# Splits of the local attention's results moved to other steps of the latent attention

## The chip, the cores and the metric

The kernel runs on one core of a Trainium2 chip. A core has five engines that work side by side, each through its own list of instructions in order: TensorE (PE in the profile, with PEld for its weight loads), VectorE (DVE), ScalarE (ACT), GpSimd (POOL) and SyncE (SP), which here issues nearly all transfers between HBM and the on-chip memory SBUF. Matmul results go to PSUM banks, which DVE and ACT read. Engines wait for each other through semaphores. The metric is the device time of one execution in microseconds (us); the time before is 1336.53 us, the median of three runs.

## The reference

One decoder block on a sequence of 1024 positions with a model width of 1024, all in float32. Two attentions run side by side and are mixed:

```
h = RMSNorm(x); p = h @ w_in          # queries, keys, values, latents, gates
A = sliding-window attention (window 128, 8 heads, 2 key/value heads, sinks, rotary)
B = multi-head latent attention (8 heads, low-rank q and kv, causal, blocks of 128 queries)
y = sigmoid(gate_a) * (A @ w_o_swa) + sigmoid(gate_b) * (B @ w_o_mla)
x = x + y @ w_out
x = x + SwiGLU(RMSNorm(x)); final RMSNorm
```

The change concerns `A @ w_o_swa`, the output product of the local (sliding-window) attention. The kernel computes it during the latent attention.

## The kernel before, in words

Every large matrix product is made of three matmuls on float32r operands (`mm3`, L168 to L174): each operand is split into a high part, the value rounded by a cast, and a low part, the rest. `split` (L160 to L166) is one cast on ACT (L163) and one subtraction on DVE (L166). So each matmul operand that does not come out split costs ACT and DVE one instruction each per 128x512 piece.

The local attention leaves its result in HBM as `oa_d`, four pieces of 128x1024 (a group `g` of channels and a half `sh` of the sequence each). `load_oa(g, sh)` (L1261) takes buffers and issues the load of one piece into `oar`; `split_oa(g, sh, c)` (L1265) splits one half of the piece, 128x512, into `wv`, where the output product (`mix_a`, `oA` in the profile) reads it. There are four loads and eight splits in all. The weights of that product come through `wr` and are split into another `wv` of 128x1024.

Latent attention first makes its operands: key products (`prod_k`, `k`), query products (`prod_q`, `q`) and value blocks (`prod_v`, `v`). Then it runs 64 steps, eight heads by eight blocks of 128 queries in the order 2, 3, 6, 7, 0, 1, 4, 5. Step t is written like this:

1. `scores(t + 2)` (L1180 to L1208): the matmuls of two steps ahead into `scb` (two PSUM slots), the masked row maximum `nmb` on DVE (L1204), the exponential `p` on ACT (L1205), and on POOL the reciprocal `denb` (L1206) and the scaling of `p` (L1207).
2. The products of probabilities and values (`pv`, `ob`) that have become due.
3. In steps 0 to 3 one of the four last key products, (2, 0) to (3, 1), whose split result `kns` is stored to `kn_d` and loaded again for later heads. In steps 5 and 6, and in some of each later head's, half an output product `mix_a`.
4. `transposes(t)`: PE transposes `p` into `pTb`, which is split into `pth` and `ptl`.
5. Loads and splits for the output products: the part that the change touches.

Steps 0 and 1 have their scores before the loop. The whole order of PE, ACT, DVE and SP in this stage is not the written one: outside of the stretches that are marked as written by hand, a scheduler sets each engine's order when the program is built, from the written order and estimated times, with casts inside the loop's last part held in their written order among each other (`held`). The order then stands fixed in each engine's list, and each engine waits at the head of its list.

Before the loop, `load_oa(0, 0)` and `load_oa(1, 0)` stand ahead of the last query product `prod_q(3, ...)`. `ps1` has four PSUM banks that `q`, `k`, `v`, `pTb`, `ob` and `oA` share.

Of the kernel before, what the change touches and what calls it, by code (L numbers as in the profile page):

```python
# [89 lines left out]
def hybrid_block_kernel(  # L90
# [39 lines left out]
    def psum_phase(name, bufs):  # L130
        if psum:
            psum.pop("cm").close()
        psum["cm"] = ExitStack()
        psum["x"] = psum["cm"].enter_context(tc.tile_pool(name=name, bufs=bufs, space=PSUM))
# [9 lines left out]
    def U(name, dt=F32, shape=(P, 1024)):  # L144
        return pool.tile(list(shape), dt, tag="u", name=uid(name))

    def V(name, dt=F32, shape=(P, 4, 512)):
        return vpool.tile(list(shape), dt, tag="v", name=uid(name))
# [12 lines left out]
    def split(hi, lo, src, eng=None):  # L161

        i = nc.scalar.copy(hi, src)  # L163
        if held[0]:
            tc.keep_in_program_order(i)
        (eng or nc.vector).tensor_tensor(lo, src, hi.bitcast(F32), op=ALU.subtract)  # L166

    def mm3(ps, pairs, first=True, last=True, go_on=False):  # L168

        n = len(pairs)  # L170
        for i, ((ah, al), (bh, bl)) in enumerate(pairs):
            nc.tensor.matmul(ps, ah, bh, start=first and i == 0, stop=False, skip_group_check=go_on)  # L172
            nc.tensor.matmul(ps, ah, bl, start=False, stop=False, skip_group_check=go_on)  # L173
            nc.tensor.matmul(ps, al, bh, start=False, stop=last and i == n - 1, skip_group_check=go_on)  # L174
# [10 lines left out]
    def half(s):  # L185
        return slice(512 * s, 512 * s + 512)
# [189 lines left out]
    for g in range(NG):  # L376
        t = V("khd", F32R, (P, 2, S))
# [486 lines left out]
    for b in range(NB):  # L864
# [17 lines left out]
        t = U("lat", F32, (P, C_CKV))  # L882
# [100 lines left out]
    for i, b in enumerate((4, 5, 6, 7, 0, 1, 2, 3)):  # L983
        ps = P1("kl", (P, KVL))
        mm3(ps, [(hT(k, blk(b)), (wkl[k // 4][0][:, k % 4], wkl[k // 4][1][:, k % 4])) for k in range(NK)])
        t = U("lat", F32, (P, 2, KVL))
# [137 lines left out]
    def prod_q(j, s, k0=0, n=3):  # L1124
        w = wuq[j]
        if k0 == 0:
            q_ps[0] = (P1 if j > 1 else PX)("q")
        ps = q_ps[0]
        mm3(ps, [((w[:, 0, k], w[:, 1, k]), (cq[k][0][:, half(s)], cq[k][1][:, half(s)])) for k in range(k0, k0 + n)],
            k0 == 0, k0 + n == 3)  # L1130
        if k0 + n < 3:
            return
        t = U("qns", F32R, (P, 2, 512)) if j else None
        outs = [(t[:, 0], t[:, 1], ps)] if j else [
            (qT[u][0:64, 0, half(s)], qT[u][0:64, 1, half(s)], ps[64 * u:64 * u + 64]) for u in range(2)]
        for hi, lo, src in outs:
            nc.scalar.activation(hi, src, AF.Copy, scale=-SC_B)
            nc.vector.scalar_tensor_tensor(lo, src, -SC_B, hi.bitcast(F32), op0=ALU.mult, op1=ALU.subtract)
        if j:
            nc.sync.dma_start(qn_d[j][:, :, half(s)], t.bitcast(F32))  # L1140
# [13 lines left out]
    def prod_v(b):  # L1154
        ps = P1("v")
        mm3(ps, [((ckv[k][0][:, blk(b)], ckv[k][1][:, blk(b)]), (wv[0][:, k], wv[1][:, k])) for k in range(2)])
        if b % 2 == 0:
            t = V("vM", F32R, (P, 2, NH, P))
            vM.extend([t[:, 0], t[:, 1]])
        split(vM[b][:, :, 0:HD], vM[b][:, :, HD:P], ps.rearrange("p (h d) -> p h d", d=HD))  # L1160

    def load_k(h):
        nc.sync.dma_start(kT[h % 3][0:64].bitcast(F32), kn_d[h // 2, 64 * (h % 2):64 * (h % 2) + 64])
# [16 lines left out]
    def step(t):  # L1180
        return t // NB, order[t % NB]

    def scores(t):
        h, n = step(t)
        w = (n + 1) * P
        sc = PX("scb", (P, 1024))
        qh, ql = (qT[h][0:QK, i] for i in range(2))
        kh, kl = (kT[h % 3][0:QK, i] for i in range(2))
        cw = 320 if w == 640 else 512
        for c0 in range(0, w, cw):  # L1190
            c1 = min(c0 + cw, w)
            kc = slice(c0, c1)
            o = slice(c0 // cw * 512, c0 // cw * 512 + c1 - c0)
            nc.tensor.matmul(sc[:, o], qh[:, blk(n)], kh[:, kc], start=True, stop=False)
            nc.tensor.matmul(sc[:, o], qh[:, blk(n)], kl[:, kc], start=False, stop=False)
            nc.tensor.matmul(sc[:, o], ql[:, blk(n)], kh[:, kc], start=False, stop=True)  # L1196
        nm = tiny("nmb")
        p = U("p")
        den = tiny("denb")
        s_, m_, p_ = sc[:, 0:w], mask[:, S - w:], p[:, 0:w]  # L1200
        if cw == 320:
            s_ = sc.rearrange("p (a c) -> p a c", a=2)[:, :, 0:320]
            m_, p_ = (v.rearrange("p (a c) -> p a c", a=2) for v in (m_, p_))
        nc.vector.tensor_tensor_reduce(s_, s_, m_, 1.0, -NEG, op0=ALU.add, op1=ALU.min, accum_out=nm)  # L1204
        nc.scalar.activation(p_, s_, AF.Exp, scale=-1.0, bias=nm, accum_out=den)  # L1205
        nc.gpsimd.tensor_tensor(den, den, neg_one[:, 0:1], op=ALU.pow)  # L1206
        nc.gpsimd.tensor_scalar(p[:, 0:w], p[:, 0:w], den, 0.0, op0=ALU.mult, op1=ALU.add)  # L1207
        live[t] = p  # L1208
# [16 lines left out]
    def pv(h, j):  # L1225
        tiles = pts.pop((h, j))
        js = []
        for q in order:
            if q % 2:
                js.append(q // 2)  # L1230
        i = js.index(j)
        first = i % 2 == 0
        pair = sorted(js[i // 2 * 2:i // 2 * 2 + 2])
        slot = pair.index(j)
        if first:
            po_live[h] = P1("ob", (P, 2, 256))
        po = po_live[h][:, slot]
        nk = 2 * j + 2
        for kb in range(nk):
            q_off = P if kb == nk - 1 else 0  # L1240
            hi, lo = tiles[kb // 4]
            vst = vM[kb][:, h]
            nc.tensor.matmul(po[:, q_off:], vst, hi[:, kb % 4, q_off:], start=kb == 0, stop=False)
            nc.tensor.matmul(po[:, q_off:], vst, lo[:, kb % 4, q_off:], start=False, stop=kb == nk - 1)
        if not first:
            po = po_live[h]
            tmp = U("otb")
            tv = tmp[0:64, 0:512].rearrange("p (a c) -> p a c", a=2)
            nc.scalar.copy(tv, po[64:128])
            if h % 2 == 0 and i == 1:  # L1250
                ob[h // 2] = U("ob")
            r = (h % 2) * 64
            ov = ob[h // 2][r:r + 64].rearrange("p (a c) -> p a c", a=4)
            ov = ov[:, pair[0]:pair[1] + 1:pair[1] - pair[0]]
            nc.vector.tensor_tensor(ov, po[0:64], tv, op=ALU.add)
# [9 lines left out]
    def split_oa(g, sh, c):  # L1265
        raw, (hi, lo) = oa_raw[(g, sh)] if c == 0 else oa_raw.pop((g, sh))
        split(hi[:, c], lo[:, c], raw[:, c])
        oaT[(2 * g + c, sh)] = (hi[:, c], lo[:, c])
# [77 lines left out]
    nc.vector.memset(mask[:, 0:S - P], 0.0)  # L1346
    nc.vector.tensor_scalar(mask[:, S - P:], band[:, P:], -1.0, None, op0=ALU.mult)
    prod_q(3, 0)
    prod_q(3, 1)
    psum_phase("psb", 2)  # L1350
    prod_v(4)
    scores(0)
# [15 lines left out]
    for t in range(NT):  # L1368
        h, n = divmod(t, NB)
        if t + 2 < NT:  # L1370
            scores(t + 2)
        while pvq and pvq[0][0] <= t:
            pv(*pvq.pop(0)[1:])
        if n == 4 and h + 2 < NH:
            load_q(h + 2)
        if n == 6 and h + 3 < NH:
            load_k(h + 3)
        hh, nn = step(t)
        if nn % 2 == 1:
            pvq.append((t + 3, hh, nn // 2))  # L1380
        e = t - (NT - 8)
        if e == 6:
            psum_phase("psc", 4)
        if t in first:
            prod_k(*first[t])
        if t in fill:
            dc, sh, c0 = fill[t]
            mix_a(dc, sh, c0, 2, P1("oA") if c0 == 0 else None)
        if t == NT - 1:
            mix_a(13 // 2, 13 % 2, 0, 4, PX("oA"))  # L1390
        transposes(t)
        held[0] = True
        if t == 3:
            load_oa(0, 1)
            load_oa(1, 1)
        if t < 4 or 6 <= t < 10:
            split_oa(t % 4 // 2 if t < 4 else (t - 6) // 2, t // 6, t % 2)
        if t + 6 in w_at or t == 0:
            st.load_to(st.index[("oa", w_at.get(t + 6, 0))])
        if t + 2 in w_at:  # L1400
            st.conv_to(st.index[("oa", w_at[t + 2])])
        if e == 4:
            load_sigs(DCS[0])
        if -3 <= e < 3:
            split_ob((e + 3) // 2, (e + 3) % 2)
        if e in (2, 6):
            st.load_to(st.index[("ob", 2 if e == 2 else 0)])
        if e == 6:
            st.conv_to(st.index[("ob", 2)])
        held[0] = False  # L1410
# [482 lines left out]
```

## Time and profile before

| | |
|---|---|
| median of three runs | 1336.53 us (1336.42 to 1337.27) |
| the profiled execution | 1336.93 us, of which the span is 1335.1 us |
| clock granted to PE, mean | 0.998 |
| PE, DVE, ACT, POOL busy | 99%, 68%, 48%, 42% of the span |
| latent attention's scores | from 376.7 to 546.3 us of the span |
| splits of `oar` | casts from 389.9, subtractions from 391.7, last ones at 415.5 and 416.2 us |

A row of the timeline is: start, duration, engine, line, operation, output<-inputs, sizes, count, and in brackets the idle time of the engine ahead of it with what ended that. PE overlaps its matmuls, so its rows overlap: a full-width matmul starts every 0.23 us and is shown with 0.39. Rows of the DMA issues show the time of the issue at SP; the time to landing is given apart. All times are microseconds from the span's start.

### The profile page before, as it was taken

The page shows a single profiled execution, that of the slowest core. Times are in us where ns is not written, and L with a number is a line of the kernel's source. Part 1 is how long each engine was busy: PE and PEld are TensorE (multiplying, and loading weights), DVE is VectorE, ACT ScalarE, POOL GpSimd, SP SyncE. Part 2 cuts the span into 40 slices and gives each one's busy share as a digit, 9 for nine tenths or more (in the row PEclk, how much of TensorE's full clock was granted, in tenths as well). Part 3 has the DMA queues.
Part 4 walks back from the last instruction along what each step waited for, and adds up shares of the span by engine and source line. Part 5 has one row for each costly group of instructions (what it writes and reads, how often), then busy time and mean ns, then how long its engine had stood idle before and what let it go on. Part 6 is the DMA issues. An engine that isn't in the chain of part 4 may idle for free. (4 is left out here: it accounts for less than half of the span.)

```text
span 1335.1 us, 19045 instructions
## 1 busy us (share of the span) xinstructions
PE 1323.6 (99%) x6564; PEld 1115.3 (84%) x6564; DVE 904.6 (68%) x1471; ACT 636.5 (48%) x1291; POOL 567.0 (42%) x614
## 2 busy tenths in 40 slices
PE   9999999999999999999999999999999999999997
PEld 6899888888888889888887888888888888888886
DVE  7868777776767767696469766666665654664862
ACT  7434676675556766753335323322233233644443
POOL 2115556552325554451131765755666541022521
PEclk9999999999999999999999999999999999999999
DMA  9454322335575530681532354534443425996504
GB/s 376 154 188 163 108 104 83 119 115 193 160 246 151 111 95 17 252 291 56 222 129 91 143 182 172 200 133 181 181 162 142 169 95 191 386 381 223 174 16 142
DMA packets 85311, 223.61 MB, mean 167 GB/s; under 512 B 9632, under 2 KB 16288, under 8 KB 84128
## 3 DMA queue, kind: packets, MB, share of 16 engines
q1 hardware_dynamic: 83776, 220.05, 47.1%
q10 hardware_dynamic: 1440, 2.36, 0.5%
q8 instruction: 52, 0.85, 0.3%
q14 instruction: 43, 0.35, 0.1%
HBM read 151.72 MB, written 70.12 MB: 166 GB/s over the span
## 5 line engine op out<-in xcount | busy, mean ns | idle before, releaser
L166 DVE TENSOR_TENSOR wl<-wr,wl 128x512 fp32r<-128x512 f32 x150 | 148.7, 1015 | 71.2 <-ACT wl L163 70.9
L166 DVE TENSOR_TENSOR lrv<-lr,lrv 128x1024 fp32r<-128x1024 f32 x77 | 105.1, 1396 | 49.0 <-ACT lrv L163 46.4
L163 ACT CAST lrv<-lr 128x1024 fp32r<-128x1024 f32 x77 | 80.1, 1052 | 95.6 <-PE fd L174 69.5
L172 PE MATMUL fd<-lrv 128*128 128x512 f32 x308 | 119.8, 389 | 0.0
L173 PE MATMUL fd<-lrv 128*128 128x512 f32 x308 | 119.8, 389 | 0.0
L174 PE MATMUL fd<-lrv 128*128 128x512 f32 x308 | 119.8, 389 | 0.0
L177 POOL TENSOR_TENSOR wr<-wr,sm 128x512 f32<-128x512 f32 (+1 forms) x38 | 45.8, 1213 | 162.6 <-DVE wl L166 136.2
L163 ACT CAST wl<-wr 128x512 fp32r<-128x512 f32 x150 | 87.0, 623 | 1.4 <-DVE wr L835 1.1
L1206 POOL TENSOR_TENSOR denb<-denb,neg_one 128x1 f32<-128x1 f32 x64 | 40.1, 627 | 96.2 <-ACT p L1205 84.4
L166 DVE TENSOR_TENSOR wl<-sm,wl 128x512 fp32r<-128x512 f32 x60 | 48.2, 829 | 42.2 <-ACT wl L163 42.1
L173 PEld LDWEIGHTS fd<-lrv 128*128 128x128 f32 x308 | 57.8, 188 | 12.1
L174 PEld LDWEIGHTS fd<-lrv 128*128 128x128 f32 x308 | 57.8, 188 | 12.0
L172 PEld LDWEIGHTS fd<-lrv 128*128 128x128 f32 x308 | 57.8, 188 | 11.9
L311 POOL TENSOR_SCALAR ms<-ss 128x1 f32<-128x1 f32 x32 | 8.9, 277 | 138.0 <-ACT xn L1652 61.1
L1205 ACT ACTIVATE p<-scb,nmb 128x384 f32<-128x384 f32 (+3 forms) x64 | 47.8, 747 | 33.3 <-DVE nmb L1204 25.6
L166 DVE TENSOR_TENSOR ptl<-pTb,pth 128x512 fp32r<-128x512 f32 (+2 forms) x96 | 50.5, 551 | 16.6 <-ACT pth L163 16.2
L1204 DVE CUSTOM_DVE_ANT_0 scb<-scb,mask 128x384 f32<-128x384 f32 (+3 forms) x64 | 48.5, 760 | 15.0 <-PE scb L1196 13.0
L1537 ACT ACTIVATE act<-sm 128x512 f32<-128x512 f32 x11 | 7.0, 632 | 104.4 <-DVE sm L180 104.4
L1207 POOL TENSOR_SCALAR p<-p,denb 128x384 f32<-128x384 f32 (+3 forms) x64 | 48.0, 749 | 6.3
L1537 ACT ACTIVATE act<-pu 128x512 f32<-128x512 f32 x22 | 13.9, 633 | 70.6 <-DVE pu L180 70.6
L163 ACT CAST pth<-pTb 128x512 fp32r<-128x512 f32 (+2 forms) x96 | 43.5, 482 | 8.5 <-PE pTb L1221 7.5
L172 PE MATMUL fb<-t2h,wl 128*128 128x512 f32 x120 | 47.4, 395 | 0.0
(356 smaller groups left out, 4319.1 us busy)
## 6 DMA issues: line engine op xcount, KB each, us to landing
lr<-la_d SPq DMA_DIRECT2D x77, 256.0 KB, 5.4
wr<-in_w_gate_dram SPq DMA_DIRECT2D x22, 512.0 KB, 4.2
wr<-in_w_up_dram SPq DMA_DIRECT2D x22, 512.0 KB, 5.0
wd<-in_w_down_dram SPq DMA_DIRECT2D x22, 512.0 KB, 6.9
rb_d<-wd SPq DMA_DIRECT2D x22, 512.0 KB, 2.7
la_d<-sd SPq DMA_DIRECT2D x22, 512.0 KB, 5.7
lr<-rb_d SPq DMA_DIRECT2D x44, 256.0 KB, 5.4
lr<-in_w_down_dram SPq DMA_DIRECT2D x33, 256.0 KB, 5.4
```

Of the source, the lines that this page charges most:

```text
L163: i = nc.scalar.copy(hi, src)
L166: (eng or nc.vector).tensor_tensor(lo, src, hi.bitcast(F32), op=ALU.subtract)
L172: nc.tensor.matmul(ps, ah, bh, start=first and i == 0, stop=False, skip_group_check=go_on)
L173: nc.tensor.matmul(ps, ah, bl, start=False, stop=False, skip_group_check=go_on)
L174: nc.tensor.matmul(ps, al, bh, start=False, stop=last and i == n - 1, skip_group_check=go_on)
L177: eng.tensor_tensor(out, a, b, op=ALU.subtract)
L311: nc.gpsimd.tensor_scalar(ms, ss, 1.0 / width, EPS, op0=ALU.mult, op1=ALU.add)
L1204: nc.vector.tensor_tensor_reduce(s_, s_, m_, 1.0, -NEG, op0=ALU.add, op1=ALU.min, accum_out=nm)
L1205: nc.scalar.activation(p_, s_, AF.Exp, scale=-1.0, bias=nm, accum_out=den)
L1206: nc.gpsimd.tensor_tensor(den, den, neg_one[:, 0:1], op=ALU.pow)
L1207: nc.gpsimd.tensor_scalar(p[:, 0:w], p[:, 0:w], den, 0.0, op0=ALU.mult, op1=ALU.add)
L1537: nc.scalar.activation(dst, src, AF.Silu)
```

## The change

The four splits of the pieces (0, 0) and (1, 0) are written ahead of the loop, between and behind the two last query products, where they were in steps 0 to 3. The loads of (0, 1) and (1, 1) are written in step 0, where they were in step 3, and their four splits in steps 1 to 4, where they were in steps 6 to 9. The splits ahead of the loop are not held in written order.

```
     prod_q(3, 0)
+    split_oa(0, 0, 0)
+    split_oa(0, 0, 1)
     prod_q(3, 1)
+    split_oa(1, 0, 0)
+    split_oa(1, 0, 1)
     psum_phase("psb", 2)
...
         transposes(t)
         held[0] = True
-        if t == 3:
+        if t == 0:
             load_oa(0, 1)
             load_oa(1, 1)
-        if t < 4 or 6 <= t < 10:
-            split_oa(t % 4 // 2 if t < 4 else (t - 6) // 2, t // 6, t % 2)
+        if 1 <= t < 5:
+            split_oa((t - 1) // 2, 1, (t - 1) % 2)
```

What the scheduler makes of it is seen in the order of the engines. POOL's list stays the same. On ACT, ahead of step 0 (`p` is the exponential, the first one is step 0's, the second step 1's), before:

```order
L163 CAST vM_4225<-v_4256 128x8x64
L163 CAST vM_4312<-v_4305 128x8x64
L1137 ACTIVATE qns_4283<-q_4273 128x512
L1137 ACTIVATE qns_4297<-q_4287 128x512
L1205 ACTIVATE p_4320,denb_4321<-scb_4315,nmb_4319 128x384
L163 CAST kns_4333<-k_4326 128x512
L163 CAST kns_4344<-k_4337 128x512
L1205 ACTIVATE p_4353,denb_4354<-scb_4348,nmb_4352 128x512
L163 CAST vM_4312<-v_4359 128x8x64
L163 CAST vM_4375<-v_4368 128x8x64
```

and changed:

```order
L163 CAST vM_4225<-v_4256 128x8x64
L1137 ACTIVATE qns_4283<-q_4273 128x512
L1137 ACTIVATE qns_4301<-q_4291 128x512
L163 CAST wv_4266<-oar_4265 128x512 x2
L163 CAST wv_4269<-oar_4268 128x512 x2
L163 CAST vM_4320<-v_4313 128x8x64
L1205 ACTIVATE p_4328,denb_4329<-scb_4323,nmb_4327 128x384
L163 CAST kns_4341<-k_4334 128x512
L163 CAST kns_4352<-k_4345 128x512
L163 CAST vM_4320<-v_4367 128x8x64
L163 CAST vM_4383<-v_4376 128x8x64
L1205 ACTIVATE p_4361,denb_4362<-scb_4356,nmb_4360 128x512
```

The two last query casts now stand ahead of the fourth value block's, the four casts of `oar` follow them, and step 1's exponential stands two value casts later. DVE has the same pieces in much the same places: two subtractions of `oar` ahead of step 0's maximum, two behind it.

On ACT from step 2's exponential (128x896) to step 5's (128x256), before:

```order
L1205 ACTIVATE p_4396,denb_4397<-scb_4388,nmb_4395 128x896
L163 CAST kns_4409<-k_4402 128x512
L163 CAST pth_4413<-pTb_4415 128x3x128
L163 CAST wv_4266<-oar_4265 128x512
L163 CAST pth_4413<-pTb_4450 128x4x128
L163 CAST wv_4266<-oar_4265 128x512
L1205 ACTIVATE p_4433,denb_4434<-scb_4425,nmb_4432 128x1024
L163 CAST kns_4446<-k_4439 128x512
L1205 ACTIVATE p_4464,denb_4465<-scb_4459,nmb_4463 128x128
L163 CAST kns_4477<-k_4470 128x512
```

and changed:

```order
L1205 ACTIVATE p_4404,denb_4405<-scb_4396,nmb_4403 128x896
L163 CAST kns_4417<-k_4410 128x512
L163 CAST pth_4421<-pTb_4423 128x3x128
L163 CAST pth_4421<-pTb_4462 128x4x128
L1205 ACTIVATE p_4445,denb_4446<-scb_4437,nmb_4444 128x1024
L163 CAST kns_4458<-k_4451 128x512
L163 CAST wv_4430<-oar_4429 128x512
L1205 ACTIVATE p_4476,denb_4477<-scb_4471,nmb_4475 128x128
L163 CAST kns_4489<-k_4482 128x512
L163 CAST pth_4493<-pTb_4497 128x4x128
L163 CAST pth_4495<-pTb_4504 128x3x128
L163 CAST wv_4430<-oar_4429 128x512
```

Two casts of the first pair are gone from between the transposed blocks, and the first cast of the second pair stands between step 3's key cast and step 4's exponential. On DVE, in the same place, the first of these key blocks (`kns`) and step 0's transposed block now stand ahead of step 3's maximum (128x1024), where they stood behind it:

```order
L1204 ISA scb_4396,nmb_4403<-scb_4396,mask_4048 128x896
L1204 ISA nmb_4403 128x1
L166 TENSOR_TENSOR kns_4417<-k_4410,kns_4417 128x512
L166 TENSOR_TENSOR ptl_4422<-pTb_4423,pth_4421 128x3x128
L1204 ISA scb_4437,nmb_4444<-scb_4437,mask_4048 128x1024
```

That is the changed order; the subtraction into `kns_4417` is what SP's store of it waits for.

On SP, from the store of that key block on, before:

```order
L1152 DMA kn_d<-kns_4409 256x1x512
L238 DMA wr_4423<-in_w_o_swa_dram 128x1024
L1152 DMA kn_d<-kns_4446 256x1x512
L1152 DMA kn_d<-kns_4477 256x1x512
L1263 DMA oar_4536<-oa_d 128x1024
L1152 DMA kn_d<-kns_4518 256x1x512
L1263 DMA oar_4539<-oa_d 128x1024
L1168 DMA qT_4570<-qn_d 64x2048
```

and changed:

```order
L1152 DMA kn_d<-kns_4417 256x1x512
L1263 DMA oar_4429<-oa_d 128x1024
L1263 DMA oar_4432<-oa_d 128x1024
L238 DMA wr_4435<-in_w_o_swa_dram 128x1024
L1152 DMA kn_d<-kns_4458 256x1x512
L1152 DMA kn_d<-kns_4489 256x1x512
L1168 DMA qT_4576<-qn_d 64x2048
L1152 DMA kn_d<-kns_4530 256x1x512
```

The two loads stand ahead of the weight load and of two key stores. On PE no matmul is added or removed; in steps 1 to 8 some scores, key products, transposes and value products change places, the first ones being step 1's scores, now between the two key products (1, 0) and (1, 1), and step 6's scores, now behind the last key product.

## The prediction

> **What bounds the kernel now.** I read the page's busy shares first, then who waited for whom on TensorE, then the stretches, then the engines' timelines around the place that the change touches.
>
> ```profile
> span 1335.1 us, 19045 instructions
> PE 1323.6 (99%) x6564; PEld 1115.3 (84%) x6564; DVE 904.6 (68%) x1471; ACT 636.5 (48%) x1291; POOL 567.0 (42%) x614
> ```
>
> TensorE (PE) is busy for 99% of the span, and the change leaves its matmuls as they are. Time can only come from its waits, and only where moved work ends them. Its waits between 360 and 560 us, from latent attention's query products to its end, are these:
>
> ```profile
> PE scb L1194 <- ACT p L1205: 1.1, 3, 0.6
> PE oA L173 <- DVE wv L166: 0.5, 1, 0.5
> PE oA L174 <- DVE wv L166: 0.3, 1, 0.3
> ```
>
> Together 1.9 us. That is the most that the stage can give back while PE does the same work, and it is less than 0.2% of the time (2.7 us), which is about what a measurement of this kernel can tell from no change. The stretches (busy us of PE, PEld, DVE, ACT, POOL with counts, then clock and DMA) show where there is room:
>
> ```profile
> 370.00:375.00 5.00, 5.00 (x24) 4.14 (x23) 1.38 (x2) 1.19 (x2) 0.00 (x0) 1.00 0.93 324
> 375.00:380.00 5.00, 5.00 (x25) 4.21 (x24) 2.15 (x5) 1.58 (x3) 0.00 (x0) 1.00 0.49 179
> 395.00:400.00 5.00, 5.00 (x35) 4.39 (x34) 5.00 (x10) 4.56 (x10) 2.34 (x5) 1.00 0.81 274
> 410.00:415.00 5.00, 4.70 (x28) 4.12 (x29) 4.71 (x8) 3.25 (x9) 3.18 (x4) 1.00 0.44 93
> 415.00:420.00 5.00, 4.48 (x31) 3.69 (x30) 4.65 (x10) 4.09 (x12) 3.05 (x4) 1.00 0.04 17
> ```
>
> Ahead of 380 us VectorE (DVE) and ScalarE (ACT) are busy for less than half; from 390 to 420 us DVE is nearly full, and there PE loses time. The moved work and its loads:
>
> ```profile
> L163 ACT CAST wv<-oar x8: 623/642/662, 389.9 to 415.5; 128x512 fp32r<-128x512 f32 x8
> L166 DVE TENSOR_TENSOR wv<-oar,wv x8: 678/681/1364, 391.7 to 416.2; 128x512 fp32r<-128x512 f32 x8
> 372.20 1.49 SPq L1263 DMA_DIRECT2D oar<-oa_d  x2
> 396.69 0.80 SPq L1263 DMA_DIRECT2D oar<-oa_d  x1
> 399.58 0.61 SPq L1263 DMA_DIRECT2D oar<-oa_d  x1
> oar<-oa_d SPq DMA_DIRECT2D x1, 512.0 KB, 4.8
> oar<-oa_d SPq DMA_DIRECT2D x1, 512.0 KB, 5.4
> oar<-oa_d SPq DMA_DIRECT2D x1, 512.0 KB, 7.2
> ```
>
> Eight casts, eight subtractions, four loads. The 4.8 and 5.4 us are the first two loads', issued at 372.20 and some 0.7 later; the last one, issued at 399.58, took 7.2. Nothing is added or removed.
>
> **Part 1: four splits ahead of step 0.** In both kernels their loads go out at 372.2 and 372.9, so they land at 377.0 and 378.3.
>
> ```profile
> 377.10 0.59 ACT L163 CAST vM<-v 128x512 fp32r<-128x512 f32 x1 [4.85 <-PE v L174]
> 377.58 1.10 ACT L1137 ACTIVATE qns<-q 128x512 fp32r<-128x512 f32 x2
> 381.23 0.58 ACT L1205 ACTIVATE p<-scb,nmb 128x384 f32<-128x384 f32 x1 [2.55 <-issue]
> 382.74 0.71 ACT L1205 ACTIVATE p<-scb,nmb 128x512 f32<-128x512 f32 x1
> 380.53 0.56 DVE L1204 CUSTOM_DVE_ANT_0 scb<-scb,mask 128x384 f32<-128x384 f32 x1
> 381.05 0.70 DVE L1204 CUSTOM_DVE_ANT_0 scb<-scb,mask 128x512 f32<-128x512 f32 x1
> 382.22 0.39 PE L172 MATMUL v<-wv,ckv 128*128 128x512 f32 x1
> 387.82 0.48 PE L1194 MATMUL scb<-kT,qT 96*128 96x512 f32 x1
> 390.68 0.60 PE L1221 MATMUL pTb<-ident,p 128*128 128x128 f32 x4
> ```
>
> Before, ACT stands 4.85 us in front of the fourth value block's cast, with two ready query casts behind it, and 2.55 us more in front of step 0's exponential. The order shown with the change puts the query casts first and the four splits' casts next. Two casts in a row start 0.55 apart (1.10 for two), so ACT casts at 377.0 to 379.5 and does the value block by 380.0. DVE subtracts twice, takes step 0's row maximum (0.5) and is done with it at 379.5. Step 0's exponential can start at 380.0, a little earlier than its 381.23. Step 1's maximum now stands behind two more subtractions, the value block and both key blocks, five at 0.6: 382.5 for 381.05. Its exponential stands behind a value cast that waits for PE until 383.7: 384.3 for 382.74, 1.6 later. Those who wait for it are step 3's scores, which reuse its banks (387.82), and step 1's transposes (390.68): slack 2.8 us or more. The other user is the PSUM bank of the fourth value block, free now at 381.3; the sixth block's matmuls want it at 382.22, slack 0.9. Cost of part 1: nothing, covered by these slacks. If the second load landed 0.9 us later than its 5.4, PE would begin to wait, one for one.
>
> **Part 2: four splits in steps 1 to 4, their loads in step 0.** The loads stood behind two key stores (396.69 and 399.58); now SP issues them right behind the first key store. Who waits there:
>
> ```profile
> 391.35 0.52 SPq L1152 DMA_DIRECT2D kn_d<-kns  x1
> 390.63 0.69 DVE L166 TENSOR_TENSOR kns<-k,kns 128x512 fp32r<-128x512 f32 x1
> 393.42 0.58 ACT L163 CAST kns<-k 128x512 fp32r<-128x512 f32 x1
> 393.94 0.37 ACT L1205 ACTIVATE p<-scb,nmb 128x128 f32<-128x128 f32 x1
> 394.45 0.42 PE L1194 MATMUL scb<-kT,qT 96*128 96x320 f32 x1 [0.26 <-ACT p L1205]
> 397.72 0.36 PE L1243 MATMUL ob<-pth,vM 128*128 128x256 f32 x1
> ```
>
> That store waits for a subtraction which DVE now does ahead of step 3's maximum (1.23 us) instead of behind it: it ends at about 389.8, not 391.3. Issue follows at 390.4 and 391.1. With 4.8 us the first lands at 395.2. But ACT meets its cast right behind the key cast (393.42 now, 392.9 without the two split casts ahead of it), so at 393.4: it stands idle 1.8 us, with step 4's exponential behind it (395.7 for 393.94), a key cast, step 2's two transposed blocks and step 5's exponential. PE feels it at step 6's scores, which need the banks that step 4's exponential reads. The change puts a key product (six matmuls, 1.4 us) ahead of them, so they come at 395.4 and wait until 396.05 (0.6); step 3's transposes then wait for the bank of the late key block (0.85) and for one another's copies (0.15). Less the 0.26 that was there, and what the new order saves between, PE reaches the first probability-times-value product at 398.7 instead of 397.72: **1.0 us behind**.
>
> **Part 3: steps 6 to 9 are free of splits.**
>
> ```profile
> 409.47 0.69 ACT L1205 ACTIVATE p<-scb,nmb 128x512 f32<-128x512 f32 x1 [0.31 <-DVE nmb L1204]
> 410.30 0.50 PE L1194 MATMUL scb<-kT,qT 96*128 96x512 f32 x1 [0.63 <-ACT p L1205]
> 417.60 0.50 PE L173 MATMUL oA<-wv,wv 128*128 128x512 f32 x1 [0.52 <-DVE wv L166]
> 414.02 1.36 DVE L166 TENSOR_TENSOR wv<-oar,wv 128x512 fp32r<-128x512 f32 x1
> 416.22 1.33 DVE L166 TENSOR_TENSOR wv<-oar,wv 128x512 fp32r<-128x512 f32 x1
> 415.89 1.12 POOL L1207 TENSOR_SCALAR p<-p,denb 128x1024 f32<-128x1024 f32 x1
> ```
>
> ACT loses four casts there (2.2 us) and DVE four subtractions (0.68 twice, 1.36 and 1.33: 4.1 us). That is more than the lateness of part 2. So step 9's exponential goes at about 409.7 as before, and PE, which waited 0.63 for it, comes late enough not to wait (the other 0.3 are pieces of 0.1 that PE lost between 400 and 410 to the old order): 410.4 against 410.30, **0.1 behind**. The 0.52 at 417.60 was a wait for a moved subtraction, now done ten us earlier. Sum: 1.0 − 0.9 − 0.5 = **−0.4 us**.
>
> Two of the eight subtractions took twice as long, 1.36 and 1.33 for 0.68; the second began while GpSimd's (POOL's) scaling ran (415.89 to 417.01) and ended 0.54 after it. The four ahead of step 0 cannot meet this, since POOL has nothing to do until step 0's exponential. The four in steps 1 to 4 can, at 0.65 to 0.7 each, where DVE is full; my estimate is none to two collisions, and in steps 0 to 3 before none of four was longer than 0.68. The Trainium skill ("SBUF — State Buffer", section "SBUF: two separate sides") says that VectorE with two SBUF inputs and GpSimd take a shared port pair as an exclusive lock, the loser blocked for the whole instruction; these two rows agree. By that rule a collision costs what is left of the scaling, at most the 1.12 us of the longest one, so two of them on the path would make the sum −0.2 + 2.2 (1338.5) where two at 0.7 make it −0.2 + 1.4 (1337.7, below); either is within 0.2%.
>
> **Bounds.** The one unknown that matters is when the second pair lands: 4.8 (the neighbours are alike: one store ahead, another load behind) to 7.2 us. At 7.2 everything from 395 us on is 2.4 later, and with nothing recovered the sum is −0.4 + 2.4 = +2.0. If ACT never blocks, all 1.9 us of waits can go. I take 5.0, near the first pair, since the queue there is most like the new place: −0.4 + 0.2 = **−0.2 us**. The profiled execution took 1336.93 us (span 1335.1 and 1.8 around it), 0.40 above the median 1336.53; it would become 1336.7, and the median **1336.3**.
>
> **Rivals.**
> - *The waits go and no new one comes* (the pair lands before ACT reaches its cast). For it: ACT and DVE are ahead of the old schedule up to step 3. Against: the load would have to be issued 1.8 us earlier or land in 3 us, and none of the four landed under 4.8. Time: 1336.5 − 1.9 = 1334.6.
> - *POOL collides with the subtractions in steps 1 to 4.* Two collisions on a full DVE, +1.4: −0.2 + 1.4, so 1337.7. For it: two of eight did so before; against: none in the same steps.
> - *Slower: ACT stands in front of the cast in step 1 for long.* Every exponential, key cast and transposed block from step 4 on is queued behind that one cast, PE's scores behind them. Price one for one; it decides from a landing of 7.9 us (−0.4 + 3.1 = +2.7). For it: a query load issued 0.6 us after the 7.2 us one took longer still:
>
> ```profile
> qT<-qn_d SPq DMA_DIRECT2D x1, 512.0 KB, 8.4
> ```
>
>  Against: that one stood right behind the 7.2 us load, and the new place is like the first pair's. With such a landing, 8.4, the time is 1336.5 − 0.4 + 3.6 = 1339.7.
>
> **How the numbers follow.** Near cancellation 0.62, at 1336.3 with its own range 1335.6 to 1337.4; waits gone 0.12; POOL collisions or a landing of 6 to 7 us 0.14; the slower rival 0.12. Faster than 0.2% would need more than all of PE's waits here, 0.02 kept for what I overlook, out of the first rival's share. So 0.02 faster, 0.86 same, 0.12 slower. The range that leaves out no more than two in ten reaches from the gone waits, 1334.7, to a landing of about 7.5 us, 1338.7.
>
> **What would show it.** In the changed profile: the casts of the first pair between 377 and 380 us and ACT's two long waits there gone; an ACT wait of 1 to 2.5 us for the load of the second pair near 394 us; PE waiting about 1.5 us in all between 394 and 399 us for step 4's exponential and a key subtraction; no PE wait near 410 and 417 us. I would be wrong if PE waits more than 3 us between 376 and 410 us, if the value block's bank holds PE at 382 us, or if the order of another stage has moved.

## The result and the profile after

The changed kernel took 1339.3 us (median of 19 runs, 1337.89 to 1341.82), the kernel before 1337.33 us beside it (19 runs, 1336.09 to 1339.46). The ratio is 1.0015, with a 95% interval of 1.0008 to 1.0022: about 2.0 us slower, where 0.2 us faster was forecast and 1338.7 us was the range's upper end. The profiled execution took 1338.39 us, its span 1336.6.

Who waited for whom on TensorE (PE) from 360 to 560 us in the changed kernel (us in total, times, longest):

```profile
PE scb L1194 <- ACT p L1205: 1.7, 2, 1.5
PE pTb L1221 <- DVE kns L166: 0.7, 1, 0.7
PE pTb L1221 <- ACT ar L1300: 0.7, 1, 0.7
PE oA L174 <- DVE wv L166: 0.3, 1, 0.3
```

Before, the sum was 1.9 us, spread over five places. Now it is 3.4, and 2.2 of it lies at one place, the stretch from 395 to 400 us (busy us of PE, PEld, DVE, ACT, POOL, then clock and DMA; 415 to 420 us below it):

```profile
395.00:400.00 5.00, 2.82 (x15) 1.97 (x15) 2.41 (x6) 3.06 (x8) 1.50 (x3) 1.00 0.87 325
415.00:420.00 5.00, 5.00 (x35) 4.43 (x35) 3.33 (x7) 3.78 (x10) 3.87 (x6) 1.00 0.02 3
```

PE worked through that stretch before and is idle for 2.2 us of it now; from 415 to 420 us, where it lost half a microsecond before, it is now full. Both halves of the forecast's picture are there, the loss larger than it said. ScalarE's (ACT's) timeline shows whose wait it is, and SyncE's (SP's) queue below it when the load went out:

```profile
378.21 2.37 ACT L163 CAST wv<-oar 128x512 fp32r<-128x512 f32 x4 [1.27 <-DMA oar<-oa_d]
...
393.47 0.59 ACT L163 CAST kns<-k 128x512 fp32r<-128x512 f32 x1
396.94 0.62 ACT L163 CAST wv<-oar 128x512 fp32r<-128x512 f32 x1 [2.88 <-DMA oar<-oa_d]
397.47 0.36 ACT L1205 ACTIVATE p<-scb,nmb 128x128 f32<-128x128 f32 x1
397.82 0.57 ACT L163 CAST kns<-k 128x512 fp32r<-128x512 f32 x1
398.29 0.97 ACT L163 CAST pth<-pTb 128x512 fp32r<-128x512 f32 x2
```

```profile
390.54 0.52 SPq L1152 DMA_DIRECT2D kn_d<-kns  x1
391.10 1.48 SPq L1263 DMA_DIRECT2D oar<-oa_d  x2
392.67 0.42 SPq L238 DMA_DIRECT2D wr<-in_w_o_swa_dram  x1
```

The third load went out at 391.10 and its data were there 5.8 us later. ACT stood 2.88 us in front of it, with step 4's exponential (128x128), a key cast and two transposed blocks behind.

The profiled executions do not start this stage at the same moment, so distances are counted from PE's first scores of step 0 (scb, 96x384). For the kernel before, these are PE's first scores, a score group near 418 us and the stage's last probability-times-value product:

```profile
376.90 0.34 PE L1194 MATMUL scb<-kT,qT 96*128 96x384 f32 x1
418.42 0.36 PE L1194 MATMUL scb<-kT,qT 96*128 96x256 f32 x1
557.37 0.22 PE L1243 MATMUL ob<-pth,vM 128*128 128x128 f32 x1
```

And for the changed one, with its waits:

```profile
377.50 0.34 PE L1194 MATMUL scb<-kT,qT 96*128 96x384 f32 x1
...
397.97 0.42 PE L1194 MATMUL scb<-kT,qT 96*128 96x320 f32 x1 [1.48 <-ACT p L1205]
399.38 0.63 PE L1221 MATMUL pTb<-ident,p 128*128 128x128 f32 x4 [0.70 <-DVE kns L166]
400.74 0.28 PE L1243 MATMUL ob<-pth,vM 128*128 128x256 f32 x1
...
410.53 0.85 PE L1221 MATMUL pTb<-ident,p 128*128 128x128 f32 x6 [0.69 <-ACT ar L1300]
413.11 0.48 PE L1194 MATMUL scb<-kT,qT 96*128 96x512 f32 x1
...
420.23 0.36 PE L1194 MATMUL scb<-kT,qT 96*128 96x256 f32 x1
559.06 0.22 PE L1243 MATMUL ob<-pth,vM 128*128 128x128 f32 x1
```

Distances after minus before: at the first product ob +2.4 us (23.24 for 20.82), at the scores of 413.11 +2.2 (35.61 for 33.40), at the 96x256 scores +1.2 (42.73 for 41.52), at the stage's last product +1.1 (181.56 for 180.47). So PE fell 2.4 behind where 1.0 was forecast, and won 1.3 back where 1.4 was. Of the 2.0 us in the timed runs this execution shows 1.1; the third profile below shows what some executions have besides.

### The profile page after: what moved, and what is told of

It reads as the page before. It is cut to its first block, busy times and chain, and to the rows that moved or that the text cites. A ratio compares the mean times of both kernels' runs of the same rounds, so it can differ in the third digit from the quotient of the medians.

```text
span 1336.6 us, 19041 instructions
## 1 busy us (share of the span) xinstructions
PE 1323.3 (99%) x6564; PEld 1115.2 (83%) x6564; DVE 905.4 (68%) x1471; ACT 636.1 (48%) x1291; POOL 568.5 (43%) x614
```

## The experiments

Theory A: the loss is ACT's stand in front of the third load. Theory B: it is the splits' work on VectorE (DVE) in steps 1 to 4, and its collisions with GpSimd. Theory C: it is the four splits ahead of step 0. "Stage" is the distance from step 0's first scores to the stage's last ob, and "first ob" that to the first ob, each minus the value before (180.47 and 20.82); both come from one profiled execution. "Stand" is ACT's wait for the third load. Ratios are of timed runs, eleven of each kernel here (nine of the second-pair-alone one), with the kernel before beside them.

| kernel | ratio to before, 95% interval | stage, us | first ob, us | stand, us |
|---|---|---|---|---|
| changed, again | 1.0011 (1.0002 to 1.0020) | +1.3 | +2.7 | 3.14 |
| changed, third time | 1.0014 (1.0005 to 1.0022) | +2.0 | +3.4 | 2.91 |
| first pair alone | 0.9991 (0.9983 to 1.0000) | −1.0 | −0.6 | none |
| second pair alone | 1.0029 (1.0019 to 1.0039) | +4.4 | +5.7 | 3.67 |
| second pair loaded ahead of step 0 | 0.9979 (0.9970 to 0.9988) | −2.0 | 0.0 | none |
| loads ahead of the key store | 0.9996 (0.9987 to 1.0005) | +0.6 | +2.8 | 1.17 |
| fourth load in step 1 | 0.9997 (0.9988 to 1.0005) | +0.2 | +2.1 | 2.81 |
| both loads in step 1 | 1.0016 (1.0007 to 1.0025) | +3.7 | +4.0 | 4.19 |
| loads in step 0, splits in 6 to 9 | 0.9996 (0.9987 to 1.0004) | 0.0 | −0.1 | none |
| loads in step 0, splits in 3 to 6 | 0.9988 (0.9979 to 0.9997) | −1.9 | −0.1 | none |
| loads ahead of step 0, splits in 6 to 9 | 0.9989 (0.9980 to 0.9998) | −0.5 | 0.0 | none |
| loads ahead of step 0, splits in 0 to 3 | 0.9991 (0.9982 to 0.9999) | −1.1 | +0.7 | none |

All edits are to the changed kernel.

**The changed kernel again.** No edit.

> The changed kernel once more, beside which the others of this set are read. Against the kernel before it took 2.0 us more (ratio 1.0015); about +1 to +2.7 us is expected again. Its trace should again show ScalarE waiting 2 to 3 us for the third load of the local results (oar) near 394 to 397, and TensorE waiting some 1.5 us for step 4's exponential and 0.7 us for the key cast (kns) behind it.

Slower by 1.5 us (0.3 to 2.7, by the ratio), with a stand of 3.14 us and PE waiting 1.73 and 0.70 us behind it. The loss is no accident of one execution.

**Only the first pair moved.**

```diff
-        if t == 0:
+        if t == 3:
             load_oa(0, 1)
...
-        if 1 <= t < 5:
-            split_oa((t - 1) // 2, 1, (t - 1) % 2)
+        if 6 <= t < 10:
+            split_oa((t - 6) // 2, 1, t % 2)
```

> Only the first pair of results is split ahead of step 0; the second pair is loaded in step 3 and split in steps 6 to 9, as in the kernel before. Theory A (ScalarE stands in front of the third load in step 3, with step 4's exponential and its key cast queued behind) : no such stand here, so 0 to 0.7 us below the kernel before, some 2 to 2.7 us below the changed one. Theory B (the splits' work on VectorE and their collisions with GpSimd in steps 1 to 4 cost the time): the same direction here, 0 to 0.7 below before. Theory C (the four splits ahead of step 0 cost it): as the changed kernel, +1.5 to +2.5 us over before.

1336.31 us for 1337.38: theory C falls. Part 1 does not cost time; it gains about 1 us (the interval just reaches no change), which the forecast had at nothing and the expectation above at 0.7 us at most. PE's waits, 360 to 560 us:

```profile
PE scb L1194 <- ACT p L1205: 0.6, 2, 0.4
PE oA L173 <- DVE wv L166: 0.5, 1, 0.5
PE oA L174 <- DVE wv L166: 0.3, 1, 0.3
```

With the first pair's casts out of steps 0 to 3, the first ob comes 0.6 us sooner; the 0.5 us wait for the last split, step 9's, is still there.

**Only the second pair moved.**

```diff
     prod_q(3, 0)
-    split_oa(0, 0, 0)
-    split_oa(0, 0, 1)
     prod_q(3, 1)
-    split_oa(1, 0, 0)
-    split_oa(1, 0, 1)
...
         if 1 <= t < 5:
             split_oa((t - 1) // 2, 1, (t - 1) % 2)
+        if t < 4:
+            split_oa(t // 2, 0, t % 2)
```

> The first pair is split in steps 0 to 3 as in the kernel before; the second pair is loaded in step 0 and split in steps 1 to 4 as in the changed one, so steps 1 to 3 hold two splits. Theory A: the stand of ScalarE is there, with the first pair's waits as well: +2 to +4 us over before. Theory B: two splits a step, so twice the collisions: +2.5 to +5 us. Theory C: the splits ahead of step 0 are gone, so no more than +0.5 us over before.

1341.74 us, 4.4 over before (3.9 by the ratio): the slow part is the second pair, and theory C falls again. Theories A and B both expected about that. What PE waits for, and ACT's cast:

```profile
PE pTb L1221 <- DVE kns L166: 3.7, 1, 3.7
PE k L172 <- DVE kns L166: 0.6, 1, 0.6
```

```profile
397.92 0.62 ACT L163 CAST wv<-oar 128x512 fp32r<-128x512 f32 x1 [3.67 <-DMA oar<-oa_d]
```

**The same splits, loaded sooner.** This separates A from B: ACT, DVE and GpSimd do the same splits in steps 1 to 4, only the data are there.

```diff
     split_oa(1, 0, 0)
     split_oa(1, 0, 1)
+    load_oa(0, 1)
+    load_oa(1, 1)
     psum_phase("psb", 2)
...
-        if t == 0:
-            load_oa(0, 1)
-            load_oa(1, 1)
```

> The changed kernel with the two loads of the second pair issued ahead of step 0; its splits stay in steps 1 to 4 with the same instructions on ScalarE, VectorE and GpSimd. Theory A: ScalarE no longer waits for the load (2.88 us of waiting gone), TensorE's waits of 1.48 and 0.70 us near 398 are gone, and the time is 0 to 1.5 us below the kernel before. Theory B: the waiting for the load is gone, but the time stays +1 to +2 us over before, since the VectorE work in these steps is the same. Theory C: +1.5 to +2.5 us over before.

1335.09 us, ratio 0.9979 (0.9970 to 0.9988): faster than before and than the changed kernel, and by more than the 0 to 1.5 us that theory A expected. Theory B falls with it as the cause of the loss. SP's queue, ACT's first cast of the third load, with no stand ahead of it, and PE's waits:

```profile
373.59 2.00 SPq L1263 DMA_DIRECT2D oar<-oa_d  x3
379.08 0.59 SPq L1263 DMA_DIRECT2D oar<-oa_d  x1
```

```profile
393.19 0.62 ACT L163 CAST wv<-oar 128x512 fp32r<-128x512 f32 x1
```

```profile
PE scb L1194 <- ACT p L1205: 0.5, 2, 0.2
PE oA L174 <- DVE wv L166: 0.3, 1, 0.3
```

0.8 us of waits are left of 1.9. PE reaches the first ob exactly as before (20.83 for 20.82) and gains 2.0 us behind it, 1.5 of them because steps 6 to 9 are free (the early loads with splits in 6 to 9, below, lack that much).

**Loads just ahead of the key store.** A smaller dose: the two loads move one place up SP's queue.

```diff
+        if t == 0:
+            load_oa(0, 1)
+            load_oa(1, 1)
         if t in first:
             prod_k(*first[t])
...
-        if t == 0:
-            load_oa(0, 1)
-            load_oa(1, 1)
```

> The changed kernel with one thing moved: in step 0 the two loads of the second pair stand on SyncE's queue just ahead of the store of the keys (kn_d<-kns) instead of just behind it; all else is in the changed kernel's order. The loads should go out right behind the kT load, near 388.1 instead of 391.1, and with a landing of 5.8 us be there at 394, when ScalarE comes to the cast. Theory A (ScalarE's stand is the whole loss): the stand falls from 2.88 us to 0.3 or less and the time is 1.5 to 2.3 us below the kernel before, as with the loads ahead of step 0. Theory B (the loads themselves, wherever they stand in these steps, slow the kernel): still above the kernel before.

A miss: 0.1 us under before by the medians, not 1.5 to 2.3, and the interval holds no change, so it is not shown to be above before either, as theory B had it. The stand fell to 1.17 us, but the order now has this cast ahead of step 3's exponential, and PE waited 1.05 and 0.21 us for exponentials. What came then was new. ACT's wait, the stretches, and one of PE's next matmuls:

```profile
395.43 0.62 ACT L163 CAST wv<-oar 128x512 fp32r<-128x512 f32 x1 [1.17 <-DMA oar<-oa_d]
```

```profile
396.00:398.00 2.00, 0.78 (x5) 0.42 (x3) 0.98 (x4) 2.00 (x7) 0.67 (x2) 1.00 1.07 422
398.00:400.00 2.00, 1.96 (x8) 1.72 (x9) 2.00 (x5) 2.00 (x5) 1.89 (x3) 0.74 0.20 76
400.00:402.00 2.00, 2.00 (x6) 1.44 (x6) 2.00 (x5) 0.32 (x2) 1.12 (x2) 0.50 0.89 337
402.00:404.00 2.00, 2.00 (x18) 2.00 (x17) 1.38 (x5) 1.87 (x4) 0.00 (x0) 0.91 1.11 337
```

```profile
399.66 0.63 PE L173 MATMUL k<-ckv,wv 128*128 128x512 f32 x1
```

The granted clock (the figure behind POOL's) fell to 0.50 for about 3.4 us, and a 128x512 matmul took 0.63 us instead of 0.39. PE counts as busy there, so no list of waits shows it: up to the first ob it is busy for 22.31 us with the matmuls that took 20.57 before, which is 1.7 of the 2.8 us that it is behind there.

**Fourth load one step later.**

```diff
-        if t == 0:
-            load_oa(0, 1)
-            load_oa(1, 1)
+        if t < 2:
+            load_oa(t, 1)
```

> The changed kernel with the fourth load moved from step 0 to step 1, so that on SyncE's queue the load of the weights (wr) stands between the third and the fourth. It asks why the third load took 5.8 us to land. If it shared the transfer engines with the fourth one issued 0.75 us behind it: the landing falls to about 4.8 us, ScalarE's stand to about 1.9 us, and the time is some 1 us below the changed kernel, 0.3 to 1 us over the kernel before. If not (another 512 KB transfer, the wr load, follows it just as closely): landing, stand and time as in the changed kernel, +1.2 to +2 us over before.

The landing did not shrink (issued at 392.88, ACT goes on at 399.01), and the stand is as long as in the changed kernel. Yet the time is 0.8 us under before by the medians, in an interval that holds no change, and not 1.2 to 2 over. The order explains part of it: step 4's exponential now stands ahead of the cast (ACT, then PE):

```profile
395.71 0.39 ACT L1205 ACTIVATE p<-scb,nmb 128x128 f32<-128x128 f32 x1
...
399.01 0.62 ACT L163 CAST wv<-oar 128x512 fp32r<-128x512 f32 x1 [2.81 <-DMA oar<-oa_d]
```

```profile
397.71 0.50 PE L172 MATMUL k<-ckv,wv 128*128 128x512 f32 x1 [0.31 <-DVE kns L166]
401.10 1.22 PE L1221 MATMUL pTb<-ident,p 128*128 128x128 f32 x8 [1.75 <-DVE kns L166]
```

PE did its next scores in the meantime. The same idle time of ACT costs less with one exponential fewer behind it: PE is 2.1 us behind at the first ob, not 2.4 or more. PE's wait of 0.69 us for `ar` is gone as well, and no clock fall is in this profile. What each of these is worth was not separated.

**Both loads one step later.** A larger dose.

```diff
-        if t == 0:
+        if t == 1:
             load_oa(0, 1)
             load_oa(1, 1)
```

> The changed kernel with both loads of the second pair written in step 1 instead of step 0, so that the wr load stands ahead of them on SyncE's queue and the fourth load also behind the next store of the keys. A larger dose of the same wait. Theory A: the third load lands 0.6 us later or more, ScalarE stands 3.5 us or longer, and the time rises by as much or more over the changed kernel: +2 to +4 us over before. Theory B or C (VectorE's work in these steps, or the splits ahead of step 0): unchanged against the changed kernel, +1.2 to +2 us over before.

1340.97 us, 3.0 over the kernel before by the medians, but 2.1 by the ratio, hardly more than the changed kernel's 1.5 to 2.0. So the timed runs alone do not separate theory A from B and C, which expected no change against the changed kernel; the profile does (stage +3.7), though it is one execution, the slowest of the eleven. In it the stand was 4.19 us, and PE then waited 3.32 us in one piece and ran at half clock for some 7 us.

**The loads in step 0, splits later.** Twice, in steps 6 to 9 and 3 to 6.

```diff
-        if 1 <= t < 5:
-            split_oa((t - 1) // 2, 1, (t - 1) % 2)
+        if 6 <= t < 10:
+            split_oa((t - 6) // 2, 1, t % 2)
```

> The changed kernel with the second pair loaded in step 0, but split in steps 6 to 9 as in the kernel before. The two loads run as in the changed kernel, and nothing waits for them. Theory A: as the kernel with only the first pair moved, 0.7 to 1.3 us below the kernel before. Theory B' (the loads' place on SyncE's queue delays the stores of the keys and what is read back from them): at least 0.5 us over that, up to the changed kernel's +1.5 to +2 us.

1337.02 us for 1338.00, 1.0 us under by the medians as A expected, though only 0.5 us by the ratio, in an interval that holds no change; and the stage is 1.0 us longer than with the first pair alone. So B' is partly right: the weights (wr), now behind two loads on SP's queue, come late for the first output product, and PE waits 0.28 us for their cast:

```profile
402.92 1.05 ACT L163 CAST wv<-wr 128x1024 fp32r<-128x1024 f32 x1 [0.50 <-DMA wr<-in_w_o_swa_dram]
```

For steps 3 to 6 the edit has 3, 7 and (t − 3) in the place of 6, 10 and (t − 6), and the half by (t − 3) % 2.

> The changed kernel with the splits of the second pair in steps 3 to 6 instead of 1 to 4; the loads stay in step 0, behind the store of the keys. The third load, there near 397, is asked for only behind step 5's exponential, near 399. Theory A: no stand of ScalarE, and only step 6 still holds one of the splits that steps 6 to 9 had: 0.8 to 2.2 us below the kernel before. Theory B: the splits fall into the steps where VectorE has most to do (the widest maxima), so not below the kernel before.

1336.05 us for 1337.79. The loads stand where the changed kernel has them; only who asks for them, and when, is different. The stage is 1.9 us shorter than before where the changed kernel's is 1.1 to 2.0 longer: the stand, with what PE loses behind it, is worth 3.0 to 3.9 us. That VectorE is full in these steps cost nothing that shows.

**All loads ahead of step 0, splits in 6 to 9 and in 0 to 3.** The early-load edit, and on top of it

```diff
-        if 1 <= t < 5:
-            split_oa((t - 1) // 2, 1, (t - 1) % 2)
+        if 6 <= t < 10:
+            split_oa((t - 6) // 2, 1, t % 2)
```

> All four loads ahead of step 0, the second pair split in steps 6 to 9 as in the kernel before. If the kernel with early loads gained its last 1.2 us over the one with only the first pair moved because steps 6 to 9 are free of splits: here 0.5 to 1.3 us below the kernel before, with TensorE's waits of 0.5 us for the halves of the projection (oA) and of 0.4 us for an exponential still there. If it gained it by the earlier loads themselves: 1.8 to 2.6 us below.

1336.19 us for 1337.79, 1.6 under, which lies between the two ranges; the waits that the first one named, 0.5 us for a half of oA and 0.4 us for an exponential, are there. Against the early loads with splits in 1 to 4 the stage is 1.5 us longer: that is what freeing steps 6 to 9 is worth.

For the splits in 0 to 3 the two loads stand further ahead, right behind the first pair's loads and ahead of `prod_q(3, 0)`, and `if t < 4: split_oa(t // 2, 1, t % 2)` takes the place of the last two lines:

> All four loads ahead of step 0, the first pair split there, the second pair in steps 0 to 3, one step sooner than in the kernel with early loads. Theory A: no stand of ScalarE and steps 4 to 9 free of splits, so as the kernel with early loads or a little better: 1.8 to 2.8 us below the kernel before, TensorE's waits from step 0 to the end of this stage at most 0.8 us in all. Theory B (splits on VectorE in these early steps cost time wherever the data is ready): above the kernel with early loads by 0.5 us or more.

1336.30 us for 1337.79: faster than before, but not by the 1.8 to 2.8 us that theory A expected; its stage is 0.9 us longer than with the early loads, as theory B's number had it. More than half of that has another cause in the trace. With four loads in a row the order put the first casts ahead of two query casts, and ACT stood 5.33 us there until 377.54; a key product then waited 0.53 us for a query subtraction at 380.14. The same kind of stand, in another place. The other 0.4 us are not accounted for, so a small cost of VectorE's work in these steps is not excluded.

**The changed kernel, third time.**

> The changed kernel a third time. Its two profiles show 1.1 and 1.3 us more than before from step 0's first scores to the stage's end, its timed runs 1.5 to 2.0 us more, and 7 of its first 19 timed runs have a mean granted clock of 0.997, which no run of the kernel before has. If TensorE's waiting at 396 to 399 lets the clock fall to half in a part of the executions (as the profile of the kernel with the loads ahead of the store shows for 3.4 us): a third to two thirds of the runs at 0.997 or below again, these about 1 to 1.5 us above the others, the median 1.2 to 2.2 us above before. If not: all runs at 0.998 or above.

1339.81 us for 1337.79. This profile caught what the other two did not, the clock at half from about 400 to 403.4 us. The stretches:

```profile
396.00:398.00 2.00, 1.03 (x5) 0.50 (x3) 0.00 (x0) 0.49 (x1) 0.00 (x0) 1.00 0.98 363
398.00:400.00 2.00, 0.76 (x4) 0.53 (x5) 1.84 (x5) 2.00 (x7) 1.06 (x2) 1.00 0.96 381
400.00:402.00 2.00, 2.00 (x11) 1.98 (x12) 1.46 (x3) 1.82 (x6) 1.01 (x2) 0.55 0.59 221
402.00:404.00 2.00, 2.00 (x11) 1.99 (x11) 1.51 (x4) 2.00 (x4) 0.44 (x1) 0.60 1.14 297
```

The stage is 2.0 us longer than before, 0.7 to 0.9 more than in the two profiles without the fall. The mean clock of the timed runs was a bad measure of it: 2 of 11 runs at 0.997 or below, where a third to two thirds were expected with falls and none without; this profiled execution, with the fall in it, has a mean of 0.998.

## Why the prediction was wrong

**The base.** 1336.53 us was the median of three runs, 1337.33 is that of nineteen. So of the 3.0 us between the 1336.3 forecast and the 1339.3 measured, 0.8 is the base and 2.2 the change: −0.2 was forecast, +2.0 measured. That is 0.15%, inside the 0.2% to which the forecast gave 0.86.

**Part 1 (costs nothing): right that it costs nothing, wrong that it gives nothing.** The casts came at 378.2 to 380.6 instead of 377.0 to 379.5: the stage began 0.6 us later, and the first load took 5.4 us for 4.8. There was no PE wait up to 395 us. Alone it gained about 1 us (ratio 0.9991, stage −1.0).

**Part 2 (1.0 us behind): this step failed.** The mechanism was the forecast's own: ACT meets its cast too soon, with the exponential and the key cast behind it, and PE waits for just these two. The size was off. The issue was forecast at 390.4 and came at 391.10, 390.5 with the later start taken off. The landing was the mis-sized term: I took 5.0 us from the first pair because the queue looked alike, and it took 5.8 (6.1 and 5.9 in the other two profiles); over five kernels with a stand, from issue to ACT's start, 5.8, 5.8, 6.0, 6.1 and 6.8. The very load that was moved had taken as long in its old place, issued at 396.69 in the kernel before, a figure that the prediction does not list beside 4.8, 5.4 and 7.2:

```profile
oar<-oa_d SPq DMA_DIRECT2D x1, 512.0 KB, 5.8
```

With it, the forecast's own sum is −0.4 + 1.0 = +0.6. ACT stood 2.88 us instead of 2.0 (1.8 with a landing of 4.8), and PE fell 2.4 us behind instead of 1.2 (1.0).

That is more than the landing's excess, so a second term was off too. PE's wait for the exponential was 1.48 us where 0.8 follows from the forecast's 0.6 and the 0.2 for a landing of 5.0; the wait for the key cast was 0.70 where it had 0.85 and 0.15. But the forecast let the new order save some 0.3 us between them (0.6 + 0.85 + 0.15 − 0.26 is 1.3, and it took 1.0). Instead PE lost 0.5 us outside the listed waits: it is 2.42 behind, and 1.48 + 0.70 − 0.26 is 1.92. Of this 0.5, 0.35 counts as busy, 20.92 us up to the first ob for matmuls that took 20.57.

And a step was missing: that much waiting can be followed by a fall of the clock, which adds 0.7 to 0.9 us to the stage. In the third profile PE was busy for 21.85 us up to the first ob, and 3.4 behind.

**Part 3 (0.9 and 0.5 back): about right.** The changed kernel won back 1.3 us, though later than forecast: 0.2 by step 11's scores, because PE waited 0.69 us for the copy of the half product (ar), which stood on ACT behind two late exponentials. The first of these waited for a maximum that stood on DVE behind the last of the four subtractions, and that one took 1.09 us instead of 0.68 while POOL scaled:

```profile
404.68 1.30 POOL L1207 TENSOR_SCALAR p<-p,denb 128x640 f32<-128x640 f32 x1
405.43 1.09 DVE L166 TENSOR_TENSOR wv<-oar,wv 128x512 fp32r<-128x512 f32 x1
```

The other two profiles of the changed kernel have it too (1.09 and 1.01). With the data ready, the same freeing of steps 6 to 9 was worth 1.5.

**The most that could be won.** The listed waits of 1.9 us are not the most that the stage can give back. The kernel with the early loads gave back 2.0 us with 0.8 of them still there, the one with splits in 3 to 6 gave back 1.9 with 1.0 there. The rest came out of PE's busy time: for the 1132 matmul records of the stage it fell from 178.6 us to 177.7 and 177.6. Where in the matmuls it lies was not followed up.

**The rivals.** "The waits go and no new one comes" is what the kernel with the early loads does: 1.9 us were forecast for it, its stage is 2.0 shorter, by luck in part, since not all the listed waits went. "ACT stands for long" had the right mechanism, but I let it decide from a landing of 7.9 us, one for one; with the clock's share it came near that at 5.8. POOL's collisions had a small part: one subtraction of the four in these steps was long, where none to two were expected, and it cost up to 0.4 us of PE's 0.69, not 0.7.

The bound from 7.2 us of landing (+2.0) gave the change that was measured by luck: the landing was 5.8, and the rest came from terms that the sum did not have.

## What to carry to other kernels

When work is moved ahead of the point at which its data arrive, price the engine that stands in order in front of it by everything queued behind, and price the landing over the whole range of alike transfers, first of all with what the moved load itself took before, not with the one that looks nearest. Move the load first and the work second: the same splits cost 2.0 us with the loads behind a store, and saved 2.3 (medians) with the loads some fifteen microseconds sooner. A wait of one or two microseconds on TensorE can cost more than itself; look at the granted clock behind it.

## What had not been expected of the hardware

The granted clock. In profiles where PE waited 3.66 and 3.32 us in one piece it fell to 0.50 for about 7 us; with 1.51 and 0.70 us of waiting, or 1.05 and 0.21, for about 3.4 us. With 1.48 and 0.70 us, 1.73 and 0.70, or 0.31 and 1.75, it did not fall. So of three executions of the changed kernel one had it and two had not, with nearly the same waits. The Trainium skill ("TensorE: Matmul & The Clock Gate", section "Part 1: The HAM clock gate (the "warmup" mystery)") describes such a gate: half or full rate by TensorE's activity in a free-running window of 3.4 us. The lengths agree, one window or two. That the fall comes by chance would fit a free-running window, but no run here shows the window's phase. The table of the Trainium skill under "Why this matters for your kernels" on that page asks for no idle gap of more than about 3 us; here 1.05 and 0.21 us of waiting stood ahead of a fall, so by these runs a gap need not be that long. How idle a window must be was not tried, nor how many of the timed runs had the fall.

Why the third load took 5.8 us or more where the first pair took 4.8 and 5.4 is open: taking the fourth load from behind it did not shorten it (6.1), but another load of 512 KB followed in its place. The first load, from much the same place in every kernel, took 4.5 to 5.5 us, so it varies from run to run as well.
